# Later turns for the first key tiles, and four query products ahead of the later keys, in the projection stage of a two-layer encoder

## The chip, the cores and the metric

The kernel runs on one core of one Trainium2 chip. Its time is that of the whole program on the device, in microseconds; less is better. Five engines work side by side, each down its own queue in order: PE (matrix products and transposes), DVE, ACT and POOL (elementwise work and reductions), and SP, which issues the DMAs. They wait for each other on semaphores only.

## The reference

Two layers over 1024 tokens of 1024 channels, float32. Layer 0 mixes tokens by grouped-query attention, layer 1 by centred pooling; each layer then attends into a memory of 256 tokens and applies a gated MLP. The change lies in the first step of layer 0:

```python
h = rmsnorm(x, attn_norm)
qkv = h @ w_qkv                      # 16 query heads, 4 key heads, 4 value heads, 64 wide
q = apply_axial_rope(rmsnorm(q, q_gain), cos, sin) * HEAD_DIM ** -0.5
k = apply_axial_rope(rmsnorm(k, k_gain), cos, sin)
```

The scores, the softmax and all the rest follow from these q, k and v.

## The kernel before, in words

**Tiles.** Tokens come in eight tiles of 128. The projection makes, for each tile t, one product of 256 columns for the four key heads, ("K", t), one for the four value heads, ("V", t), and four for the query heads, (g, t), g being the group of four heads. `QKV` (line 41) is the list of these products in PE's order; the entries ("S", n) are score products that come later. Each product multiplies the tile's 1024 channels, eight blocks of 128, as float32 split into a high and a low part: three matmuls for each block (lines 761 to 763, `mm3`), 24 in all.

**Inputs.** The left side, `hT`, is x transposed, times the gain, split in two. It comes in four chunks of tokens, `CHUNKS`: tile 0, tile 1, tiles 2 and 3, tiles 4 to 7. `plan_columns(n)` loads chunk n from the transposed copy of x (DMA, L857) and splits it (L692 on ACT for the high part, L690 on DVE for the low). `plan_rows(t)` loads the rows of tile t (L929), squares and sums them on ACT (L933) and makes the row's normaliser `first[t]` on POOL (L935, L936); whatever follows a product of tile t multiplies by it. `plan_weights(piece, s)` loads 1 MB of weights in two DMAs (L948) and splits them (L674, L954). Raw tiles all go through six buffers, `scr`. `plan_tables` builds the tables of cosines and sines times the gains from one loaded table on POOL (L903, L910), for keys early on and for queries once key tile 0 is through its head.

**Head.** A key or query product goes through `plan_head`: square (ACT, L1011), sum (DVE, L1015), reciprocal root (POOL, L734 and L736), scale (DVE, L1023), two halves of the rotation (DVE, L1030 twice, L1034), and their sum (POOL, L1038). From tile 2 on a key tile also has a difference to the key two tiles back (POOL, L1056). Then comes its **turn**: PE transposes the result (L1062 for keys, two or four transposes; L1093 for queries, two), and ACT and DVE copy it out (L674, L677).

**Order.** `main` walks through `QKV` and hands each step to a planner (`Plan`). A turn is not placed right behind its product but `LAG` = 4 products later; `todo` holds the turns that are still to come. PE's order is exactly the order of these calls. For the other engines the planner works out when each operation is due so that PE is served in time, sorts by those times, and simulates the engines with costs of its own to fix the order in which instructions are written into each queue. So a step that moves on PE also changes the queues of ACT, DVE, POOL and SP; on the chip each engine then keeps to its written order.

Before the change, chunk 2 is planned once key tile 1 is, chunk 3 once key tile 3 is, and the rows of tile t + 1 behind key tile t:

```python
LAG = 4
...
if kind == "K" and t + 1 < NT:
    if t in (1, 3):
        plan_columns(t // 2 + 2)
    plan_rows(t + 1)
todo.append((count + LAG, after))
```

PE's order before therefore begins K0 K1 V0 V1 K2, turn of K0, V2, turn of K1, K3 V3 K4, turn of K2, the query products of tiles 0 and 1 of group 0, and so on, with turns between them. Some idle transposes (`IDLE`, L976) keep PE at work before the first products.

Of the kernel before, what the change touches and what calls it, by code (L numbers as in the profile page):

```python
# [37 lines left out]
LAST = S - (NPIECE - 1) * PIECE  # L38
MIXER = ("D0", "D1", "D2", "D3", "D4", "D5", "D6", "M0", "D7", "M1", "O0", "M2", "M3", "O2", "T0", "M4", "M5", "M6", "O4",
         "T2", "M7", "O1", "O6", "M8", "T4", "M9", "O3", "T6", "O5", "T1", "O7")  # L40
QKV = (("K", 0), ("K", 1), ("V", 0), ("V", 1), ("K", 2), ("V", 2), ("K", 3), ("V", 3),
       ("K", 4), (0, 0), (0, 1), ("K", 5), (0, 2), (0, 3), ("K", 6), (0, 4), (0, 5), ("K", 7), (0, 6), (0, 7),
       *(it for n in range(24) for it in ([(1 + n // 8, n % 8), ("S", n // 4)] if n % 4 == 1 else [(1 + n // 8, n % 8)])),
       ("S", 6), ("V", 4), ("S", 7), ("V", 5), ("V", 6), ("V", 7))
LAG = 4
QN = 4
POOLED = (2, 3)
GROUPS = [(half, m) for half in range(2) for m in range(NH // 2)]
# [587 lines left out]
class Kernel:  # L636
# [140 lines left out]
    def attention(self):  # L777
# [3 lines left out]
        K, dK = [R.get() for _ in range(2)], R.get()  # L781
        V = [R.get(), None]
# [44 lines left out]
        with tc.tile_pool(name="qk", bufs=1, reuse_waits="tile") as qk, self.psum("psq", 1, 6) as self.ps:  # L827
# [12 lines left out]
            def x_tile(n, j):  # L840
                at_ = (0, 1, 2, 4)[n] + j
                return a["xt"][at_].rearrange("p (k n) -> p k n", n=CHUNKS[n][1])

            def w_tile(piece, g):
                at_ = 2 * {"K": NKV, "V": NKV + 1, "late": NKV + 1}.get(piece, piece) + g
                return w[at_].rearrange("p (a b) -> p a b", a=4)

            def plan_columns(n):
                c0, w = CHUNKS[n]
                per = D // w  # L850
                for j in range(NK // per):
                    raw = ("xT", n, j)

                    def fetch(raw=raw, j=j):
                        at[raw] = self.scr().rearrange("p (k n) -> p k n", k=per)
                        if n:
                            nc.sync.dma_start(out=at[raw], in_=x_tile(n, j))  # L857

                    def part(lo, k, raw=raw, j=j):
                        hi, lo_ = (R.v(z, 4)[:, k % 4, c0 % 512:c0 % 512 + w] for z in hT[c0 // 512][2 * (k // 4):2 * (k // 4) + 2])  # L860
                        self.hi_lo_half(lo, hi, lo_, at[raw][:, k - per * j], gcol[:, k:k + 1])

                    def begin(g):
                        if not g:
                            nc.sync.dma_start(out=gcol, in_=a["gcol"])
                            fetch()
                        k4, r = slice(4 * g, 4 * g + 4), self.scr().rearrange("p (a b) -> p a b", a=4)
                        at["wraw", "K", g] = r
                        nc.sync.dma_start(out=at[raw][:, k4], in_=x_tile(0, 0)[:, k4])
                        for k in (slice(0, 2), slice(2, 4)):  # L870
                            nc.sync.dma_start(out=r[:, k], in_=w_tile("K", g)[:, k])
                    if n:
                        plan.add("load", 1, fetch, (), [raw], [("scr", raw)])
                    else:
                        for g in range(2):
                            k = ("wraw", "K", g)
                            plan.add("load", 1.3, partial(begin, g), (), [(raw, g), k] + ["gcol"] * (not g),
                                     [("scr", k)] + [("scr", raw)] * (not g), [raw], late=-21.0 + g)
                    for k in range(per * j, per * j + per):
                        key = ("hT", n, k)  # L880
                        src = raw if n else (raw, k // 4)
                        plan.add("copy", cost[w], partial(part, 0, k), [src, "gcol"], [key], uses=[raw])
                        plan.add("add", cost[w], partial(part, 1, k), [src, key, "gcol"], [key], uses=[raw])
                    if not n:
                        plan_weights("K", 0)
# [38 lines left out]
            def plan_rows(t):  # L924
                h, junk = ("h", t), ("hjunk", t)

                def fetch():
                    at[h] = self.scr()
                    nc.sync.dma_start(out=at[h], in_=xin[t * P:(t + 1) * P, :])  # L929

                def square():
                    ss = self.stat(1, "ss")
                    nc.scalar.activation(self.psA(), at[h], AF.Square, accum_out=ss)  # L933
                    ms = self.stat(1, "ms")
                    nc.gpsimd.tensor_scalar(ms, ss, 1.0 / D, EPS, op0=OP.mult, op1=OP.add)  # L935
                    nc.gpsimd.tensor_tensor(out=first[:, t:t + 1], in0=ms, in1=self.mh[:, :1], op=OP.pow)  # L936
                plan.add("load", 1, fetch, (), [h], [("scr", h)], late={0: -1.0, 1: 5.0, 2: 3.0}.get(t, -4.0))
                plan.add("square", 1024, square, [h], [("first", t)], [("A", junk)], [h])
# [52 lines left out]
            def plan_v(t, b):  # L991
                src = lambda: at[b].rearrange("p (h c) -> p h c", h=4)

                def part(j):
                    if V[t // 4] is None:
                        V[t // 4] = R.get()
                    v = R.tiles[V[t // 4]].rearrange("p (k h c) -> p k h c", k=4, h=4)[:, t % 4]
                    self.hi_lo_half(j, v[:, :, :HD], v[:, :, HD:], src(), first[:, t:t + 1])
                own = [("first", t)]
                plan.add("copy", 360, partial(part, 0), [b] + own, [("V", t)], uses=[b], room=None if t < 4 else ("V1", 2))  # L1000
                plan.add("add", 340, partial(part, 1), [b, ("V", t)] + own, [("V", t)], uses=[b])
# [129 lines left out]
            def main():  # L1131
                todo, count = [], 0
                plan_columns(0)
                plan_columns(1)
                plan_rows(0)
                plan_tables("K")
                for it in QKV:
                    kind, t = it[0], it[-1]
                    if kind == "S":
                        plan_peaks(t)  # L1140
                        continue
                    if kind == "V":
                        if t == 0:
                            plan_weights("V", 1)
                        elif t == 4:
                            plan_weights("late", 0)
                        done = t == NT - 1
                        b = plan_gemm(it, "V" if t < 4 else "late", t, (lambda: R.put(*hT[1])) if done else (lambda: None),
                                      ("half", 8) if done else None)
                        plan_v(t, b)  # L1150
                        after = None
                    elif kind == "K":
                        after = plan_k(t, plan_gemm(it, "K", t))
                        if t == 0:
                            plan_tables("Q")
                    else:
                        g, half = it[0], t // 4
                        if not t:
                            plan_weights(g, (2, 1, 0, 1)[g])
                        ended, gives = [], 0  # L1160
                        if it == (0, NT - 1):
                            ended, gives = sets[2], 4
                        elif it == (NKV - 1, 3):
                            ended, gives = hT[0], 8
                        it = half, *it
                        after = plan_q(it, plan_gemm(it, g, t, lambda ended=ended: R.put(*ended), ("half", gives) if gives else None))
                    count += 1
                    if kind == "K" and t + 1 < NT:
                        if t in (1, 3):
                            plan_columns(t // 2 + 2)  # L1170
                        plan_rows(t + 1)
                    todo.append((count + LAG, after))
                    while todo and todo[0][0] <= count:
                        f = todo.pop(0)[1]
                        if f:
                            f()
                for _, f in todo:
                    if f:
                        f()
                plan.run()  # L1180

            with tc.manual_schedule():
                idle = self.psB()
                for _ in range(WARM):
                    nc.tensor.transpose(idle[:, :P], self.ident, self.ident)
                main()
# [1219 lines left out]
```

## Time and profile before

| | |
|---|---|
| median of three runs | 2414.16 us (2412.76 to 2416.49) |
| the profiled execution | 2419.23 us, span 2417.4 us |
| granted PE clock, mean | 0.997 |
| PE busy | 2392.6 us, 99% of the span |
| the projections | to about 160 us |

Rows of a timeline begin with the start in us from the span's start and the duration in us; then come engine, line and operation, the tile written and those read, and in brackets the time that the engine sat idle before, with what ended it. A table of stretches gives for each the busy us of each engine with the number of instructions, then the granted PE clock, the DMA engines' busy share and GB/s. A row of a group gives the count, the busy time in us, the mean of one in ns, and the idle time before them.

### The profile page before, as it was taken

The numbers are of one execution on the slowest core, as the hardware profiler recorded it, in microseconds if no ns is written. First come the engines' busy times: TensorE is split into PE (matmuls) and PEld (weight loads), VectorE is DVE, ScalarE is ACT, GpSimd is POOL, SyncE is SP. The second block draws the span as 40 slices with busy tenths as digits, with TensorE's granted clock in tenths as the row PEclk, the third lists the DMA queues.
The fourth block names the chain that finished last, engine by engine and source line by source line (L and its number), as shares of the span: only waits on it lengthen the run. The fifth ranks groups of instructions, "written<-read, shape, count | busy, mean of one in ns | idle before, by whom it ended". The sixth has DMA issues, their size and how long they took to land.

```text
span 2417.4 us, 33999 instructions
## 1 busy us (share of the span) xinstructions
PE 2392.6 (99%) x12484; PEld 1939.3 (80%) x12484; DVE 1887.3 (78%) x2689; ACT 1182.0 (49%) x1894; POOL 426.1 (18%) x465
## 2 busy tenths in 40 slices
PE   8999999999999999999999999999999999999998
PEld 8984544688998888888888888798888888887887
DVE  6789999549873798888887767987389888888875
ACT  6335556425562555455454427555255554545442
POOL 6757777410010000000000003011000000000001
PEclk9999999999999999999999999999999999999999
DMA  7000001425951234333387533696123332338852
GB/s 254 19 2 10 19 15 45 139 89 191 322 199 44 88 98 129 109 88 109 103 288 243 190 100 124 205 324 216 51 86 113 105 109 87 114 119 272 261 187 101
DMA packets 323004, 324.41 MB, mean 134 GB/s; under 512 B 32533, under 2 KB 253053, under 8 KB 322837
## 3 DMA queue, kind: packets, MB, share of 16 engines
q1 hardware_dynamic: 322837, 322.23, 41.5%
q8 instruction: 99, 1.62, 0.3%
q14 instruction: 68, 0.56, 0.1%
HBM read 234.58 MB, written 82.64 MB: 131 GB/s over the span
## 4 chain that ended last, share of the span: by engine, by line
PE 90%; DVE 3%; issue 3%; DMA 2%; POOL 1%; ACT 1%; SPq 0%; POOLq 0%; DVEq 0%; ACTq 0%
PE pB L761 23%; PE pB L763 23%; PE pB L762 22%; PE pO L1267 4%; PE pT L1225 3%; PE pA L763 3%; PE pA L761 3%; PE pA L762 3%; PE pS L799 2%; DVE R L677 1%; PE pB L330 1%; PE pS L1303 1%; PE pA L2282 0%; DMA scr<-X 0%; DMA scr<-in_ffn_w_down 0%
## 5 line engine op out<-in xcount | busy, mean ns | idle before, releaser
L761 PE MATMUL pB<-R,R 128*128 128x512 f32 (+1 forms) x2764 | 1026.0, 371 | 3.7 <-DVE scr L446 1.2
L763 PE MATMUL pB<-R,R 128*128 128x512 f32 (+1 forms) x2760 | 1018.3, 369 | 1.4 <-DVE R L677 1.2
L762 PE MATMUL pB<-R,R 128*128 128x512 f32 (+1 forms) x2764 | 1019.3, 369 | 0.2 <-DVE R L677 0.2
L761 PEld LDWEIGHTS pB<-R,R 128*128 128x128 f32 x2764 | 522.6, 189 | 95.4 <-DVE scr L446 2.5
L763 PEld LDWEIGHTS pB<-R,R 128*128 128x128 f32 x2760 | 521.8, 189 | 89.5 <-DVE R L677 3.2
L762 PEld LDWEIGHTS pB<-R,R 128*128 128x128 f32 x2764 | 522.8, 189 | 86.3 <-DVE R L677 1.2
L674 ACT ACTIVATE R<-scr 128x512 fp32r<-128x512 f32 (+3 forms) x372 | 268.7, 750 | 230.6 <-DMA scr<-Gs 59.3
L734 POOL TENSOR_SCALAR ms<-ss 128x1 f32<-128x1 f32 (+2 forms) x93 | 26.0, 280 | 1655.6 <-ACT R L742 1284.1
L677 DVE TENSOR_TENSOR R<-X,R 128x512 fp32r<-128x512 f32 x374 | 253.1, 689 | 67.8 <-ACT R L674 67.2
L677 DVE TENSOR_TENSOR R<-scr,R 128x512 fp32r<-128x512 f32 (+2 forms) x332 | 283.8, 884 | 25.7 <-ACT R L674 25.1
L674 ACT ACTIVATE R<-X 128x512 fp32r<-128x512 f32 x374 | 231.9, 630 | 133.4 <-PE pB L762 64.0
L444 ACT COPY scr<-pB 128x512 f32<-128x512 f32 x156 | 91.1, 584 | 180.1 <-PE pB L763 172.9
L805 DVE TENSOR_REDUCE nm<-pS 128x1 f32<-128x512 f32 x240 | 152.9, 684 | 18.2 <-PE pS L799 16.4
L1970 DVE TENSOR_TENSOR X<-pB,X 128x512 f32<-128x512 f32 (+1 forms) x145 | 99.4, 687 | 82.3 <-PE pB L763 81.2
L1232 ACT ACTIVATE X<-pT 128x1024 f32<-128x1024 f32 x128 | 125.2, 1023 | 76.6 <-PE pT L1225 73.0
L761 PE MATMUL pA<-R,R 128*128 128x512 f32 (+1 forms) x420 | 150.6, 358 | 0.0
L763 PE MATMUL pA<-R,R 128*128 128x512 f32 (+1 forms) x420 | 150.2, 358 | 0.0
L762 PE MATMUL pA<-R,R 128*128 128x512 f32 (+1 forms) x420 | 150.0, 357 | 0.0
L1267 PE MATMUL pO<-X,X 128*64 128x512 f32 x512 | 123.8, 605 | 0.0
L446 DVE TENSOR_TENSOR scr<-pB,scr 128x512 f32<-128x512 f32 x156 | 107.2, 687 | 11.5 <-PE pB L763 11.4
L1225 PE MATMUL pT<-R,R 64*128 64x512 f32 x768 | 104.7, 393 | 1.3 <-ACT X L1232 1.3
L1815 DVE SCALAR_TENSOR_TENSOR scr<-scr,conv 128x1023 f32<-128x1023 f32 x66 | 84.7, 1284 | 20.9 <-ACT scr L1810 18.9
(179 smaller groups left out, 2882.3 us busy)
## 6 DMA issues: line engine op xcount, KB each, us to landing
X<-in_ffn_w_up SPq DMA_DIRECT2D x82, 512.0 KB
Gs<-X SPq DMA_DIRECT2D x105, 256.0 KB
scr<-in_ffn_w_down SPq DMA_DIRECT2D x45, 512.0 KB
scr<-Gs SPq DMA_DIRECT2D x35, 512.0 KB
scr<-in_xattn_w_kv SPq DMA_DIRECT2D x32, 512.0 KB
scr<-Gs SPq DMA_DIRECT2D x42, 384.0 KB
Wt<-scr SPq DMA_DIRECT2D x44, 256.0 KB
Gs<-scr SPq DMA_DIRECT2D x42, 256.0 KB
```

What stands on the lines that cost most here:

```text
L444: self.nc.scalar.copy(out, p)
L446: self.nc.vector.tensor_tensor(out=out, in0=p, in1=out, op=OP.add)
L674: self.nc.scalar.activation(hi, src, AF.Copy)
L677: self.nc.vector.tensor_tensor(out=lo, in0=src, in1=hi.bitcast(F32), op=OP.subtract)
L761: mm(out, ah, bh, start=start, stop=False)
L762: mm(out, ah, bl, start=False, stop=False)
L763: mm(out, al, bh, start=False, stop=stop)
L805: nc.vector.tensor_reduce(NM[G][:, 2 * n + x.start:2 * n + x.stop], S, axis=AX.X, op=OP.max, negate=True)
L1225: nc.tensor.matmul(T[G, kt % 2][:, x * 512:(x + 1) * 512], left, right, start=first and (i, j) == (0, 0), stop=shifted or (not first and i ...
L1232: nc.scalar.activation(E[G, kt], T[G, kt % 2], AF.Exp)
L1267: nc.tensor.matmul(O[G][x * HD:(x + 1) * HD], V32[kt // 4][:, kt % 4, m // 4 * 2 + x], E[G, kt][:, x * 512:(x + 1) * 512], start=kt == 0, ...
L1970: nc.vector.tensor_tensor(out=x, in0=banks[b][:, c], in1=x, op=OP.add)
```

## The change

In `QKV` key tile 3 moves ahead of value tile 2, and the query products of group 0 for tiles 0 to 3 move ahead of key tiles 4 to 7, which then alternate with the query products of tiles 4 to 7. The turns of key tiles 0 to 3 come six products after their own (`EARLY`), those of all others four as before. Chunk 3 of the columns, and the rows of tile 4, are planned behind the second query product instead of behind key tile 3; the loads of the query weights thus come ahead of them in the plan. PE's order becomes K0 K1 V0 V1 K2 K3 V2, turn of K0, V3, turn of K1, three query products, turn of K2, the fourth, turn of K3, K4, the first query's turn, and so on. The set of instructions is the same. Lines of the new file behind line 1166 stand five lower.

```diff
-QKV = (("K", 0), ("K", 1), ("V", 0), ("V", 1), ("K", 2), ("V", 2), ("K", 3), ("V", 3),
-       ("K", 4), (0, 0), (0, 1), ("K", 5), (0, 2), (0, 3), ("K", 6), (0, 4), (0, 5), ("K", 7), (0, 6), (0, 7),
+QKV = (("K", 0), ("K", 1), ("V", 0), ("V", 1), ("K", 2), ("K", 3), ("V", 2), ("V", 3),
+       (0, 0), (0, 1), (0, 2), (0, 3), ("K", 4), (0, 4), ("K", 5), (0, 5), ("K", 6), (0, 6), ("K", 7), (0, 7),
...
-LAG = 4
+LAG, EARLY = 4, 6
...
                     if kind == "K" and t + 1 < NT:
-                        if t in (1, 3):
-                            plan_columns(t // 2 + 2)
-                        plan_rows(t + 1)
-                    todo.append((count + LAG, after))
+                        if t == 1:
+                            plan_columns(2)
+                        if t != 3:
+                            plan_rows(t + 1)
+                    if it == (0, 0, 1):
+                        plan_columns(3)
+                        plan_rows(4)
+                    todo.append((count + (EARLY if kind == "K" and t < 4 else LAG), after))
+                    todo.sort(key=lambda x: x[0])
```

## The prediction

> **What bounds the kernel now.** I read first the page's busy times, then the table of stretches over the projection stage, then PE's timeline where that table shows a hole.
>
> ```profile
> PE 2392.6 (99%) x12484; PEld 1939.3 (80%) x12484; DVE 1887.3 (78%) x2689; ACT 1182.0 (49%) x1894; POOL 426.1 (18%) x465
> ```
> ```profile
> core 0: us, PE busy (x) PEld busy (x) DVE busy (x) ACT busy (x) POOL busy (x), PEclk, DMA share, GB/s
> 10.00:20.00 10.00, 9.05 (x75) 8.85 (x76) 6.93 (x15) 8.20 (x19) 4.16 (x7) 1.00 0.94 346
> ...
> 60.00:160.00 100.00, 100.00 (x827) 97.14 (x826) 77.19 (x199) 29.91 (x71) 71.85 (x99) 1.00 0.04 12
> ...
> 25.53:28.94 3.41, 0.59 (x6) 0.39 (x4) 2.34 (x8) 2.54 (x6) 2.20 (x5) 1.00 0.90 300
> 28.94:32.35 3.41, 2.64 (x13) 2.64 (x14) 3.28 (x7) 2.57 (x5) 2.56 (x6) 0.50 0.34 132
> 32.35:35.77 3.42, 3.42 (x18) 3.42 (x18) 3.13 (x7) 1.93 (x5) 3.25 (x4) 0.50 0.50 161
> 35.77:39.18 3.41, 3.41 (x31) 3.41 (x31) 3.41 (x5) 1.85 (x4) 3.41 (x6) 1.00 0.70 223
> ...
> 438.50:441.95 3.45, 2.12 (x14) 0.86 (x12) 2.78 (x3) 2.11 (x5) 2.92 (x3) 1.00 0.85 298
> ```
> ```profile
> 25.84 0.28 PE L763 MATMUL pB<-T,R 128*128 128x256 f32 x1
> 29.71 0.69 PE L1062 MATMUL pB<-ident,kr 128*128 128x128 f32 x2 [3.59 <-POOL kr L1038]
> ...
> 35.32 0.60 PE L1062 MATMUL pB<-ident,kr 128*128 128x128 f32 x2
> ...
> 56.59 0.38 PE L1062 MATMUL pB<-ident,kr 128*128 128x128 f32 x2
> 56.80 0.38 PE L1062 MATMUL pB<-ident,dk 128*128 128x128 f32 x2
> 59.90 0.38 PE L1093 MATMUL pB<-ident,qn 128*128 128x128 f32 x2
> ```
>
> PE is busy 99% of the span, so only its holes can be won. In the projections there is one: after K2's product (last matmul 25.84, done about 25.96) PE waits 3.59 us for POOL's last add on key tile 0 (L1038), because K0's turn (L1062) stands next in its queue. Then the granted clock is 0.50 from 28.94 to 35.77: from K0's turn to K1's (29.71 to 35.32) one product and two transposes take 5.61. At full speed key tile 4's turn and a product take 59.90 - 56.59 = 3.31, of which two transposes are 56.80 - 56.59 = 0.21: a product is 3.31 - 0.42 = 2.89, and that stretch would take 3.10. The half clock costs 2.5. So the hole is worth 6.1 us at most, 0.25% of the run. From 36 to 160 PE is full: the next thing to be late was nothing.
>
> POOL and DVE are next, with 71.85 and 77.19 of the 100 us from 60 to 160.
>
> **The change, part by part.** PE's matmuls are the same, reordered; the built programs' later stages have the same order on every engine, so whatever is won or lost is settled by about 60 us and carried to the end.
>
> (a) K0's turn moves behind K3's and V2's products: PE reaches it at 25.96 + 2 x 2.89 = 31.7. At its old ready time (add at 28.93 + 0.72) the wait would be gone.
>
> (b) But the planner, given later due times, sets the other queues anew, and K0's chain is late too. On SP the two tiles of the third chunk of columns now stand ahead of row tile 1, the rotary table and the gains; on ACT their eight splits stand ahead of the square of row tile 0 (L933), on which K0's scale waits.
>
> ```profile
> 14.73 1.06 ACT L674 ACTIVATE R<-scr 128x1024 fp32r<-128x1024 f32 x1 [0.25 <-DMA scr<-in_attn_w_qkv]
> 15.70 1.01 ACT L933 ACTIVATE pA<-scr 128x1024 f32<-128x1024 f32 x1
> 16.65 0.19 ACT L933 ACTIVATION_READ_ACCUMULATOR pA<-scr 128x1 f32 x1
> 17.79 0.47 ACT L1011 ACTIVATE sq<-pB,first 128x256 f32<-128x256 f32 x1 [0.95 <-POOL first L936]
> ...
> 21.33 3.31 ACT L692 ACTIVATE R<-scr,gcol 128x256 fp32r<-128x256 f32 x8 [1.61 <-DMA scr<-in_xt]
> ```
> ```profile
> 17.72 1.31 POOL L903 TENSOR_TENSOR scr<-tab,gk 128x512 f32<-128x512 f32 x1
> 18.99 0.88 POOL L910 TENSOR_TENSOR scr<-tab,gk 128x128 f32<-128x128 f32 x2
> ...
> 20.86 0.19 POOL L734 TENSOR_SCALAR ms<-ss 128x4 f32<-128x4 f32 x1
> 21.13 1.02 POOL L736 TENSOR_TENSOR rs<-ms,mh 128x4 f32<-128x4 f32 x1
> 22.11 1.16 POOL L910 TENSOR_TENSOR scr<-tab,gk 128x128 f32<-128x128 f32 x2
> ```
>
> V's weights land at 14.7; at 346 GB/s a 512 KB tile takes 1.5, so the two tiles land at 16.2 and 17.7 (estimates), not before 21.33, and the splits (8 in 3.31) end at 19.5. Square of row 0, 1.15 (15.70 to 16.84, with its read-out): 20.7; POOL's two steps for it, 0.9 (they lie between 16.84 and the cosines at 17.72): 21.6; K0's square 0.5, then row 1's 1.15: 23.2; POOL 0.9: 24.1. From there POOL has all its inputs and works down its queue: K's cosines 1.31, K0's rstd 1.3, row 2's 0.8, K's four sines 2.04, K1's rstd 1.3, row 3's 0.8, K0's add 0.74: 32.4. **K0's wait** is 32.4 - 31.7 = 0.7 instead of 3.59; K1's rstd and add then make K1's turn wait about 1.2 (K2's rstd 1.3 and K1's add 0.74 stand behind K0's, with DVE's weight splits beside them).
>
> (c) The four query products follow, needing no keys. Their weights' loads go ahead of the last chunk on SP; that chunk's eight 512-column splits on DVE, needed by K4's product, now stand right ahead of the first query's scale (L1023). The place that decides is the first query's turn (L1093). In PE's queue 13 products and four key turns stand ahead of it, not 14 and five: PE saves 3.31 up to there and owes it after. So with T the end of POOL's add for that query, and 0.1 from there to PE:
>
> change = T + 0.1 + 3.31 - 59.90 + (half clock, if any).
>
> ```profile
> L736 POOL TENSOR_TENSOR rs<-ms,mh 128x4 f32<-128x4 f32 x6 | 6.6, 1099 | 0.5
> L1038 POOL TENSOR_TENSOR kr<-kr,rb 128x256 f32<-128x256 f32 x5 | 4.1, 824 | 0.8 <-DVE kr L1034 0.7
> L936 POOL TENSOR_TENSOR first<-ms,mh 128x1 f32<-128x1 f32 x6 | 4.1, 684 | 0.5
> L734 POOL TENSOR_SCALAR ms<-ss 128x4 f32<-128x4 f32 x6 | 3.2, 535 | 0.5
> L910 POOL TENSOR_TENSOR tab<-tab,gq 128x128 f32<-128x128 f32 x4 | 2.9, 764 | 0.0
> L935 POOL TENSOR_SCALAR ms<-ss 128x1 f32<-128x1 f32 x6 | 2.3, 384 | 4.8 <-ACT pA L933 4.6
> L1056 POOL TENSOR_TENSOR dk<-kr 128x256 f32<-128x256 f32 x3 | 2.2, 739 | 0.1
> ```
> ```profile
> 30.60 0.74 POOL L1038 TENSOR_TENSOR kr<-kr,rb 128x256 f32<-128x256 f32 x1 [0.68 <-DVE kr L1034]
> ...
> 41.08 1.06 POOL L734 TENSOR_SCALAR ms<-ss 128x4 f32<-128x4 f32 x1
> ...
> 43.84 1.10 POOL L935 TENSOR_SCALAR ms<-ss 128x1 f32<-128x1 f32 x1 [0.59 <-ACT pA L933]
> ...
> 47.34 0.19 POOL L935 TENSOR_SCALAR ms<-ss 128x1 f32<-128x1 f32 x1 [0.77 <-ACT pA L933]
> 47.62 0.55 POOL L936 TENSOR_TENSOR first<-ms,mh 128x1 f32<-128x1 f32 x1
> ...
> 57.26 0.74 POOL L1038 TENSOR_TENSOR qn<-qn,rb 128x256 f32<-128x256 f32 x1
> ```
>
> Before, POOL went from 26.45 to 58.0 (57.26 + 0.74) through that list: 31.55 us, with three idle gaps of 0.68 + 0.59 + 0.77 = 2.04. Worked without gaps it is 29.5. After, K4's add and difference (1.5, with spacing 1.65) drop out of it, and K's cosines, sines and K0's rstd, done before 26.45 in the old order, come in: 1.31 + 2.04 + 1.3, with spacing 4.9. So T = 24.1 + 29.5 - 1.65 + 4.9 = **56.9**.
>
> PE meanwhile: K0's turn at 32.4 takes 0.2, V3 2.9, the wait 1.2, K1's turn 0.2, three queries 8.7, K2's turn 0.4, the fourth query 2.9: 48.9. K3's turn needs POOL's second difference, in the same queue: none to 1.6 of wait; I take 1 (it only comes off the wait that follows). With that turn, 0.4, and K4's product PE stands at the query's turn at 53.2 and waits 56.9 - 53.2 = 3.7, as long as the old wait. Without half clock: 56.9 + 0.1 + 3.31 - 59.90 = +0.4.
>
> Bounds of T: the means of the group stand above the short rows by 6 x (0.535 - 0.19) for L734, 6 x (1.10 - 1.02) for L736, 5 x (0.82 - 0.74) for L1038, 6 x (0.68 - 0.55) for L936, 6 x (0.38 - 0.19) for L935 and 4 x (0.76 - 0.44) for L910: 6.3 in all. With all steps at their shortest T is 50.6; if the old gaps of 2.0 come again, 58.9. I take 56.9 because the same DVE splits stand beside the same POOL steps.
>
> (d) **The half clock comes back.** Before, a wait of 3.59 brought it on, with PE busy 0.59 in the 3.41 us ahead of the drop; at 438.50 a stretch with 2.12 busy kept the full clock. The bound lies between 1.3 and 2.8 idle in 3.41, and a wait of 3.7 is over it wherever it falls. The price: one such stretch at half rate, 3.41 x 0.45 = 1.5, to two, 3.0; the old one was 2.5. I take 2.4.
>
> The Trainium skill, TensorE: Matmul & The Clock Gate, Part 1, says half rate comes after at least one idle window of about 3.4 us, in windows that run free. The row at 25.53 does not fully agree: the clock fell after a stretch with 0.59 busy. Read strictly, a wait of 3.7 would seldom fill a window, and the sum would stay at +0.4.
>
> (e) Covers. SP: the last chunk lands later; its splits end on DVE a little ahead of K4's product, and should they be late, each us is taken from the wait at the query's turn, 3.7 deep. PSUM: V2's product needs K0's bank, free once K0 is scaled, about 27, two us ahead.
>
> **Sum**: +0.4 + 2.4 = +2.8 us. The profiled execution took 2419.23 (span 2417.4), the median of the runs is 2414.16; both move by 2.8: 2422.0 and **2417.0**. A measurement of this kernel can tell some 0.2% from no change, 4.8 us; the three runs spread over 3.7.
>
> **The rivals.**
> Faster: POOL keeps up. The old hole goes and none opens. PE without the waits in (b) and (c), 0.7 + 1.2 + 1, reaches the query's turn at 50.3: 50.3 + 3.31 - 59.90 = -6.3, 2407.9. For it: POOL's shortest rows give T = 50.6. Against: POOL was never that fast beside DVE's splits. To win over 4.8 T must stay under 51.7: 0.08.
>
> The clock holds: as forecast, but the wait at the query's turn stays short of the bound, or the page's strict rule is true: +0.4, 2414.6. Within the same class; 0.15.
>
> Slower: DVE holds POOL. The eight splits stand right ahead of the query's scale, and beside such splits POOL's steps grew (41.08: 1.06 for 0.19, DVE running a weight split). If POOL finds the old gaps again and some more, T = 59.2, and the half clock lasts two stretches, 3.0: 59.2 + 0.1 + 3.31 - 59.90 + 3.0 = +5.7, 2419.9. It decides from T + half clock = 61.3. For it: POOL's queue is in order, and any late input holds all behind it. 0.30.
>
> That the change does not move the turn can be left out: the built order has K0's turn behind V2.
>
> **How the numbers follow.** My forecast of +2.8 has 0.47, the clock that holds 0.15, slower 0.30, faster 0.08. Same is 0.47 + 0.15 = 0.62. The range: low end, T = 54 without half clock, -2.5, with a little of the faster rival and the runs' spread, 2410.5; high end, the slower rival with 1.6 of the spread, 2421.5.
>
> **What would show it.** K0's turn waits under 1.5 us at 31.7, not 3.59; no half clock around 30; a wait of 3 to 4 us for POOL's L1038 at about 53 ahead of the first L1093 (five lines lower in the new file), the clock at 0.50 behind it until about 60; from there to 160 PE full. I am wrong if that turn starts before 54 (then faster), or after 59 (then slower), or if PE has a hole after 65.

## The result, and the profile after

| | before | after |
|---|---|---|
| median of 17 runs each | 2414.12 us (2411.61 to 2418.83) | 2420.45 us (2417.84 to 2423.63) |
| ratio after / before | | 1.0023 (1.0016 to 1.0030) |
| profiled execution, span | 2419.23, 2417.4 us | 2418.70, 2416.9 us |

By the ratio the change costs 0.23%, some 5.6 us; the two medians lie 6.3 apart. The forecast was +2.8, on the right side, at half the size. The two profiled executions say the opposite: after is 0.5 us shorter. So the first thing to read is how far each trace has come at the end of the projections. The view by source line gives it for their score products (L799): durations, then the first and last start. The first row is before, the second after.

```profile
L799 PE MATMUL pA<-R,R x16: 492/498/501, 85.5 to 160.3; 64*128 64x512 f32 x16
L799 PE MATMUL pA<-R,R x16: 492/498/501, 87.3 to 162.4; 64*128 64x512 f32 x16
```

At 162.4 against 160.3 after is 2.1 us late, and 1.8 of them are there at the first of these products. So most of the loss lies ahead of 85 us. This is PE's timeline of after, cut to the four places where it waited and the matmuls ahead of the first and the last, and the stretches around the last:

```profile
31.66 0.28 PE L763 MATMUL pB<-R,R 128*128 128x256 f32 x1
33.31 0.44 PE L1062 MATMUL pB<-ident,kr 128*128 128x128 f32 x2 [1.36 <-POOL kr L1038]
...
37.47 0.44 PE L1062 MATMUL pB<-ident,kr 128*128 128x128 f32 x2 [0.84 <-POOL kr L1038]
...
50.82 0.44 PE L1062 MATMUL pB<-ident,dk 128*128 128x128 f32 x2 [0.75 <-POOL dk L1056]
...
53.67 0.28 PE L762 MATMUL pB<-T,R 128*128 128x256 f32 x1
57.23 0.69 PE L1093 MATMUL pB<-ident,qn 128*128 128x128 f32 x2 [3.17 <-POOL qn L1038]
```
```profile
53.59:57.00 3.41, 0.48 (x5) 0.27 (x3) 2.45 (x7) 0.47 (x1) 3.08 (x6) 1.00 1.00 407
57.00:60.41 3.41, 3.17 (x15) 3.18 (x16) 2.21 (x8) 2.27 (x3) 2.93 (x6) 0.50 0.07 29
60.00:160.00 100.00, 100.00 (x825) 97.14 (x824) 75.43 (x195) 30.44 (x73) 70.38 (x99) 1.00 0.05 17
```

The old hole at 26 us is gone. In its place stand short waits at the turns of key tiles 0, 1 and 3, and one of 3.17 us at the first query's turn, with one stretch at half clock behind it. From 60 to 160 PE is full, as before.

Why the keys are late shows on ACT and POOL, timelines of after:

```profile
16.55 3.31 ACT L692 ACTIVATE R<-scr,gcol 128x256 fp32r<-128x256 f32 x8 [1.26 <-DMA scr<-in_xt]
19.77 1.01 ACT L933 ACTIVATE pA<-scr 128x1024 f32<-128x1024 f32 x1
```
```profile
23.46 0.19 POOL L935 TENSOR_SCALAR ms<-ss 128x1 f32<-128x1 f32 x1 [1.63 <-ACT pA L933]
23.73 0.56 POOL L936 TENSOR_TENSOR first<-ms,mh 128x1 f32<-128x1 f32 x1
24.67 1.29 POOL L903 TENSOR_TENSOR scr<-tab,gk 128x512 f32<-128x512 f32 x1 [0.38 <-DMA gk<-in_attn_k_gain]
...
32.49 0.76 POOL L1038 TENSOR_TENSOR kr<-kr,rb 128x256 f32<-128x256 f32 x1
```

The third chunk's splits stand ahead of the square of row tile 0, and the cosines (L903) start at 24.67 instead of 17.72. Two things hold them there, almost to the same moment. POOL comes to them at 24.29, since row tile 1's normaliser, which waits for ACT, now stands ahead of them; then the gains land 0.38 later.

What remained open was 3.5 of the 5.6 us (5.6 less the 2.1 that the two traces show), and which part of the change is to blame.

### The profile page after: what moved, and what is told of

Same layout as the page of the kernel before. It is cut to its first block, busy times and chain, and to the rows that moved or that the text cites. A ratio compares the mean times of both kernels' runs of the same rounds, so it can differ in the third digit from the quotient of the medians.

```text
span 2416.9 us, 33997 instructions
## 1 busy us (share of the span) xinstructions
PE 2390.8 (99%) x12484; PEld 1937.1 (80%) x12484; DVE 1886.9 (78%) x2689; ACT 1182.0 (49%) x1894; POOL 425.2 (18%) x465
## 4 chain that ended last, share of the span: by engine, by line
PE 90%; DVE 3%; issue 3%; POOL 2%; DMA 2%; ACT 1%; SPq 0%; POOLq 0%; DVEq 0%; ACTq 0%
PE pB L761 23%; PE pB L763 22%; PE pB L762 22%; PE pO L1272 4%; PE pT L1230 3%; PE pA L763 3%; PE pA L761 3%; PE pA L762 3%; PE pS L799 2%; PE pB L330 1%; DVE R L677 1%; PE pS L1308 1%; POOL rs L736 0%; DMA scr<-in_ffn_w_down 0%; DMA scr<-X 0%
## 5 line engine op out<-in xcount | busy, mean ns | idle before, releaser
L677 DVE TENSOR_TENSOR R<-X,R 128x512 fp32r<-128x512 f32 x374 | 252.5, 687 | 67.6 <-ACT R L674 66.9
L677 DVE TENSOR_TENSOR R<-scr,R 128x512 fp32r<-128x512 f32 (+2 forms) x332 | 284.3, 885 | 23.7 <-ACT R L674 23.1
L1230 PE MATMUL pT<-R,R 64*128 64x512 f32 x768 | 105.2, 393 | 1.4 <-ACT X L1237 1.4
```

Of the source, the lines that this page charges most:

```text
L677: self.nc.vector.tensor_tensor(out=lo, in0=src, in1=hi.bitcast(F32), op=OP.subtract)
L1230: nc.tensor.matmul(T[G, kt % 2][:, x * 512:(x + 1) * 512], left, right, start=first and (i, j) == (0, 0), stop=shifted or (not first and i ...
```

## The experiments

**Before and after once more.** Both kernels unchanged, for other profiles of them.

> The kernel before, unchanged, against itself. Both theories ask how much of the gap of the medians (+6.3 us: 2420.45 against 2414.12) the two traces can show: they show +2.1 us on the tensor engine by 65 us, which stays to 490 us. Theory W (an unlucky profile): the profiled execution of before (2419.23, above all its other runs) lost more than its usual share: two half-clock stretches behind the hole at 26 us (2.5 us by the prediction), one more at 1489.8 (1.5 us) and two chance waits at 490 and 1236 us (0.66 and 0.77). Then another profile of the same kernel has its last score product of the projections (L799) 1 to 3 us earlier than 160.3 us, and fewer half-clock stretches. Rival S (it is always so): the hole at 26 us is again 3.5 to 3.7 us with two stretches behind it and the last L799 stands at 160.2 to 160.4; then the missing 3.5 us lie in later stages. Median near 2414 under both.

The ratio of before to itself is 1.0000 (0.9991 to 1.0009), the new profile's span 2409.9. Its timelines, PE and ACT:

```profile
27.36 0.44 PE L1062 MATMUL pB<-ident,kr 128*128 128x128 f32 x2 [1.65 <-POOL kr L1038]
```
```profile
19.26 3.31 ACT L692 ACTIVATE R<-scr,gcol 128x256 fp32r<-128x256 f32 x8 [0.69 <-DMA scr<-in_xt]
```

The hole is 1.65 us, not 3.59: the third chunk landed about 2 us earlier, its splits began at 19.26, not 21.33. No half clock follows, and the last score product starts at 156.8. Theory W holds: the profile that I predicted from was the odd one.

> One more profile of the kernel before, for the size of its hole at the first key's turn. Theory W (the hole follows the landing of the third chunk of columns, on which ACT's splits wait: landed and begun at 21.33, hole 3.59; at 19.26, hole 1.65): the two move together again, hole = 1.65 + 0.94 x (start of those splits - 19.26) within 0.4 us. Rival V (the hole's size has another source on POOL or DVE): it does not fit that line.

```profile
27.68 0.69 PE L1062 MATMUL pB<-ident,kr 128*128 128x128 f32 x2 [2.02 <-POOL kr L1038]
```
```profile
19.29 3.31 ACT L692 ACTIVATE R<-scr,gcol 128x256 fp32r<-128x256 f32 x8
```

The line asks for 1.68, measured 2.02: within the 0.4, but two of the three points lie together, so this is weak support. Nor did ACT wait for the chunk this time. Most of the 0.34 above the line is one POOL step ahead of the add: a normaliser (L936) took 0.85 us, 0.55 in the second profile. A stretch of half clock followed. Last score product: 157.5.

> The changed kernel, unchanged, once more. Theory W (the profiled execution of before was the odd one: its third chunk of columns landed 2 us late, and the second profile of before has a hole of 1.65 instead of 3.59 us and its tensor engine 3.6 us further at the end of the projections, 156.3 against 159.9): the changed kernel's wait at the first query's turn stands in every execution, 3 to 4 us at 53 to 58, the matmuls of the last score product of the projections (L799) again at 161 to 163, and the time 2419 to 2421.5, 5 to 7 us above before. Rival C (chance): its waits scatter as much as those of before, and a second profile has the wait at the first query's turn under 2 us and no half clock behind it; the time then reaches down to 2415.

Ratio 1.0024 (1.0015 to 1.0033), median 2419.33. The wait is there again:

```profile
56.73 0.44 PE L1093 MATMUL pB<-ident,qn 128*128 128x128 f32 x2 [3.15 <-POOL qn L1038]
```

But no half clock follows it, and the last score product starts at 160.5. So after is at 162.4 and 160.5, before at 160.3, 156.8 and 157.5. Against the two other profiles of before, mean 157.15, after is 3.4 to 5.3 us late, which is most of the gap of 5.6 to 6.3. The rest of the span, from there to the end, is 2254.5 and 2256.0 in after, 2257.1, 2253.1 and 2254.8 in before: the means differ by 0.3, but with a scatter of 4 a share of the later stages of 1 or 2 us could not be seen.

**Which part of the change.** Each part alone.

```diff
-LAG, EARLY = 4, 6
+LAG, EARLY = 4, 4        # queries_only: new order of products and new places of the loads, old turns
```

> The new order of the products, but all turns four products later, as before: EARLY = 4. Theory T (the later key turns cost the time: with later due times the planner puts the third chunk of columns ahead of the rows and the rotary table, and the keys' chain on POOL starts 5 us later): the chain starts as in before, the hole at the first key's turn is there again, 3.4 us, but no wait at the first query's turn; the time is that of before within 1 us (2413 to 2415), some 6 us below the changed kernel. Rival Q (the four query products ahead of the later keys cost it: more steps for POOL before the first query's turn, and the splits of the last chunk ahead of its scale): a wait of about 3 us at the first query's turn stays, on top of the hole at 26 us: 2419 to 2422.

2412.61, ratio 0.9995 (0.9986 to 1.0004); last score product at 158.0. There was a hole of 1.33 at the first key's turn and none at the first query's. The four query products ahead of the keys cost nothing.

```diff
 # late_turns: on the kernel before, QKV and the loads' places untouched
-LAG = 4
+LAG, EARLY = 4, 6
...
-                    todo.append((count + LAG, after))
+                    todo.append((count + (EARLY if kind == "K" and t < 4 else LAG), after))
+                    todo.sort(key=lambda x: x[0])
```

> The old order of the products and the old places of the loads, but the first four key tiles are turned six products later: EARLY = 6. Theory T: the planner puts the third chunk of columns ahead of the rows and the table here too; the keys' chain is late as in the changed kernel, the last chunk's loads stand behind it, and key tile 4's product, now right behind the turns, waits for its columns, 3 to 6 us in all: 2416 to 2420. Rival Q: with the hole at 26 us gone and nothing in its place this part alone gains: 2409 to 2412.

2420.09, ratio 1.0029 (1.0018 to 1.0039). The size is Theory T's upper end, the place isn't. PE's timeline, its two longest waits:

```profile
40.23 0.55 PE L761 MATMUL pB<-T,R 128*128 128x256 f32 x1 [1.93 <-DVE kr L1023]
...
47.40 0.58 PE L762 MATMUL pB<-R,R 128*128 128x256 f32 x1 [2.52 <-DVE R L954]
```

A product waits until DVE's late scale frees its bank, another for the query weights' splits; not for the columns. Each wait has a stretch of half clock behind it. The chain begins as in the change: POOL's cosines started at 26.55, after 2.87 us of waiting for the gains. Later turns of the four keys alone cost the whole 0.2 to 0.3%.

**Which queue.** First the planner is told of the old due times; PE keeps the order of the change.

```diff
-plan.add("scale", 2.4, both, [qn, rb], [qn] + [("kr", t)] * (kind == "K"), uses=[qn, rb])
+plan.add("scale", 2.4, both, [qn, rb], [qn] + [("kr", t)] * (kind == "K"), uses=[qn, rb], late=10.0 if kind == "K" and t < 4 else None)
```

> The changed kernel with one hint to the planner: the adds (L1038) of key tiles 0 to 3 are due 10 us after their products' place, as with turns four products later, though the turns stand six later, as in the change. The tensor engine's order is that of the changed kernel, instruction for instruction; only the other queues go back (the loads to rows, table and gains ahead of the third chunk). Theory P (the planner's later due times cost the time, not the order of the products): the first key's turn waits under 0.5 us, the first query's turn under 3, and the time is that of before or below it: 2411 to 2414.5. Rival O (the order itself costs it, since the first query's turn comes too early for POOL's sum of work): the wait at the first query's turn stays above 3 us with half clock behind it: 2417 to 2420.

2411.86, ratio 0.9991 (0.9982 to 1.0000), 7.5 us below the changed kernel run beside it (2419.33), with the same order on PE. All key turns were met without a wait, and the first query's waited 0.61:

```profile
50.53 0.44 PE L1093 MATMUL pB<-ident,qn 128*128 128x128 f32 x2 [0.61 <-POOL qn L1038]
```

So not the order of the products, but what the planner made of the later due times.

```diff
-plan.add("load", 1.1, load, (), ["tab", "gQ", "gK"])
+plan.add("load", 1.1, load, (), ["tab", "gQ", "gK"], late=2.0)
```

> The changed kernel with one other hint: the load of the rotary table and the gains is due 2 us after the plan's start. On SP it then stands ahead of the third chunk of columns again, as in before; nothing is said to the planner of the keys' adds, which stay due as late as in the change. Theory L (what costs the time is that the keys' tables load behind the third chunk of columns, so that POOL starts the cosines at 24.7 instead of 17 us and all of its queue is late): the cosines start at 17 to 18.5, the first key's turn waits under 0.5 us, the first query's turn under 2.5, and the time falls by 4 to 7 us against the changed kernel, to 2412.5 to 2416. Rival R (the order of POOL's and ACT's own queues under the later due times): the cosines start early, but the add of the first query still ends at 56 to 58; 2418 to 2421.

2414.41, ratio 1.0004 (0.9995 to 1.0012). Here the due times of the keys are as late as in the change, and only the tables' load is told to come early. ACT, POOL and PE:

```profile
15.21 1.01 ACT L933 ACTIVATE pA<-scr 128x1024 f32<-128x1024 f32 x1
```
```profile
17.66 1.30 POOL L903 TENSOR_TENSOR scr<-tab,gk 128x512 f32<-128x512 f32 x1 [0.19 <-DMA gk<-in_attn_k_gain]
```
```profile
53.14 0.44 PE L1093 MATMUL pB<-ident,qn 128*128 128x128 f32 x2 [1.73 <-POOL qn L1038]
```

Theory L's numbers came: the cosines start 7 us earlier, the first query's turn 4.1 us earlier than in the first profile of after, and the loss is gone. But the hint moved other queues too. ACT's square of row tile 0 is back ahead of the third chunk's splits, at 15.21 instead of 19.77, and POOL's cosines ahead of row tile 1's normaliser. In the trace of after the load alone held the cosines for 0.38 us only; in that order of ACT and POOL they could not have started before 24.29, and with that landing of the gains not before 24.67. By these rows it took both, the load's place and the order of ACT and POOL, and the planner moves them together. How the loss splits between them is not shown.

**What held the first query's turn.** POOL and DVE in the timeline of after, ahead of it:

```profile
52.74 0.20 POOL L734 TENSOR_SCALAR ms<-ss 128x4 f32<-128x4 f32 x1
53.02 1.02 POOL L736 TENSOR_TENSOR rs<-ms,mh 128x4 f32<-128x4 f32 x1
54.13 0.20 POOL L734 TENSOR_SCALAR ms<-ss 128x4 f32<-128x4 f32 x1
54.41 1.01 POOL L736 TENSOR_TENSOR rs<-ms,mh 128x4 f32<-128x4 f32 x1
55.50 0.19 POOL L935 TENSOR_SCALAR ms<-ss 128x1 f32<-128x1 f32 x1
55.78 0.56 POOL L936 TENSOR_TENSOR first<-ms,mh 128x1 f32<-128x1 f32 x1
56.30 0.88 POOL L1038 TENSOR_TENSOR qn<-qn,rb 128x256 f32<-128x256 f32 x1
```
```profile
52.22 0.41 DVE L1034 TENSOR_TENSOR qn<-qn,tab 128x256 f32<-128x256 f32 x1
```

The add's last operand is there at 52.63; two other queries' roots and a row's normaliser stand ahead of it, and it ends at 57.18.

```diff
-plan.add("scale", 2.9, rstd, [ss], [ss])
+plan.add("scale", 2.9, rstd, [ss] + ([f"qn{(0, 0, 0)}"] if it in ((0, 0, 1), (0, 0, 2)) else []), [ss])
```

> The changed kernel, where the planner is told that the reciprocal roots (L734, L736) of the second and third query wait for the first query's add (L1038). In POOL's queue the add then stands ahead of them, and key tile 3's add behind the first query's root. Theory O (POOL's written order holds the first query's turn: in the trace of the changed kernel the add's operands are there at 52.6 us, but two roots of other queries and a row's normaliser stand ahead of it until 56.3): the add ends at 51 to 53.5 us, the wait of 3.2 us at the first query's turn shrinks to under 1.6, no half clock behind it, and the time falls by 1.5 to 4 us against the changed kernel: 2416.5 to 2419. Rival D (DVE's eight splits of the last chunk, or POOL's sum of work, set the end of the add): the add ends at 56 to 58 as before and the time stays at 2420 to 2421.

2417.68, ratio 1.0012 (1.0003 to 1.0021): about half the loss is gone, though this interval and those of after (1.0016 to 1.0030, 1.0015 to 1.0033) overlap. The add moved even further than expected, and PE got less of it:

```profile
48.75 1.18 POOL L1038 TENSOR_TENSOR qn<-qn,rb 128x256 f32<-128x256 f32 x1 [0.69 <-DVE qn L1034]
```
```profile
54.24 0.66 PE L1093 MATMUL pB<-ident,qn 128*128 128x128 f32 x2 [1.33 <-DVE R L677]
55.34 0.58 PE L761 MATMUL pB<-R,R 128*128 128x256 f32 x1 [0.44 <-DVE qn L1023]
```

With POOL out of the way, DVE is next late, with the copy out of an earlier turn (L677), queued behind the last chunk's splits. And the half clock, which should have stayed away, came for two stretches, the second from 57.57 to 60.99:

```profile
50.75:54.16 3.41, 2.06 (x12) 1.38 (x11) 3.12 (x7) 2.75 (x6) 1.36 (x4) 1.00 0.83 281
54.16:57.57 3.41, 2.89 (x12) 2.53 (x13) 1.47 (x5) 3.05 (x6) 2.91 (x7) 0.50 0.89 278
```

So in this profile the turn starts 2.5 to 3.0 us earlier than in the two profiles of after, but the last score product, at 161.4, lies between theirs. That POOL's order held the turn is shown; the gain of an earlier add is not, beyond the median.

**The half clock.**

```diff
-                        at[b] = self.psB()[:, :256]
+                        at[b], spare = (lambda z: (z[:, :256], z[:, 256:256 + P]))(self.psB())
...
+                    for _ in range(24 if it == ("K", 4) else 0):
+                        nc.tensor.transpose(spare, self.ident, self.ident)
```

> The changed kernel with 24 idle transposes (0.107 us each, 2.6 us in all) behind key tile 4's product, in the unused half of its bank, so that the tensor engine works during its wait for the first query's add. They add no wait: the add ends about 3.3 us behind that product. Theory H (the half clock behind the wait is a cost of its own, 1.5 us in the trace of the changed kernel): no half clock at 57, and the time falls by 1 to 3 us against the changed kernel. Rival N (POOL sets the pace behind it anyway, so that the slower products only fill later waits): the clock stays up, but the time stays within 0.7 us of the changed kernel.

The transposes filled the wait (0.54 was left of it) and the clock stayed up at 57, but the median is 2419.96, ratio 1.0022 (1.0013 to 1.0030), beside 2419.33 for the changed kernel on the same chip. Rival N's number, but not by its mechanism: in the second profile of after the clock held as well. What is not paid in every execution can't show much in a median, so this run does not settle the half clock's price. The traces do better: from the start of the first query's turn to the last score product it is 105.2 us in the first profile of after, with the half clock, and 103.8 in the second and here, without it. One stretch costs 1.4 us, and POOL does not swallow it.

**A better version?**

```diff
-LAG, EARLY = 4, 6
+LAG, EARLY = 4, 5        # with late=10.0 on the keys' adds
```

> As the run before this one, with the same hint, but the first four key tiles are turned five products later instead of six. Theory P: both holes close, the first key's turn by one product of cover (2.9 us against a hole of 1.3 to 3.6) and the first query's turn because one more product stands behind it than ahead; the projections end 1 to 2 us earlier than in before: 2410.5 to 2413. Rival O: a wait of 2 us or more stays at the first query's turn or the next one: 2414 to 2418.

2413.40, ratio 0.9994 (0.9985 to 1.0003). No wait at either turn, but 0.96 at a later product for its bank.

> The changed kernel with the adds of key tiles 0 to 3 due as before, once more, to see whether it beats before as well: its ratio was 0.9991 (0.9982 to 1.0). Theory G (a real gain: the hole of 1.65 to 3.6 us at the first key's turn and the wait of 1.1 for the query weights' splits are gone, and the projections ended at 154.0 against 156.3 us): 1.5 to 3 us below before, ratio 0.9988 to 0.9994. Rival Z (chance of the first round): within 1 us of before, ratio 0.9996 to 1.0004.

2414.04, ratio 0.9999 (0.9990 to 1.0008): Rival Z. The third chunk's splits began at 20.17 in this profile, and the first query's turn waited 2.04, with a stretch of half clock behind it. The due times put back undo the loss; a gain over before is not shown.

## Why the prediction was right, and where it was off

**(a) right.** PE is through with V2 at 31.95 (31.7 forecast), where K0's turn waits.

**(b) right, with one term left out, and the heart of the matter.** The splits end at 19.86 (19.5 forecast), POOL starts the cosines at 24.67 (24.1), K0's add ends at 33.25 (32.4). The waits: K0 1.36 (0.7), K1 0.84 (1.2), K3 0.75 (1). The step came to the cosines by ACT's queue alone, which brings POOL there at 24.29. That the gains land later still, which the step had on SP's list but put at nothing, cost 0.38. The hint on the tables' load, with what it moved on ACT and POOL, brings the time to that of before.

**(c) right.** T = 57.18 (56.9 forecast); PE is there at 54.05 (53.2) and waits 3.17 (3.7). The formula gives 57.18 + 0.1 + 3.31 - 59.90 = +0.7. I summed POOL's work and overlooked that two steps of other queries need not stand ahead of the add; the sum fitted because they do.

**(d) mis-sized, and not always there.** One stretch at half rate, not 2.4 us: 2.1 at the last score product less 0.7 is 1.4. In the second profile of after there was none, with the same wait. There the clock held, as in the rival of that name. That a wait of 3.7 is over the bound "wherever it falls" did not follow from the step's own numbers: split evenly over two windows it leaves 1.85 us idle in each, within the 1.3 to 2.8 in which the step had left the bound open.

**The base was wrong**, and this is the step that failed in size: "both move by 2.8". The formula subtracts 59.90, the start of the first query's turn in the profiled execution of before. I had 2419.23 against 2414.16 on the table and took the 5 us as lying evenly on both sides. Some 3.4 of them sat ahead of that turn, in the hole and the half clock behind it. In the other two profiles of before that turn starts at 56.3 and 56.7; these are the view by source line of L1093:

```profile
L1093 PE MATMUL pB<-ident,qn x64: 270/272/273, 56.3 to 166.3; 128*128 128x128 f32 x64
```
```profile
L1093 PE MATMUL pB<-ident,qn x64: 270/272/329, 56.7 to 167.0; 128*128 128x128 f32 x64
```

With their mean the formula gives 57.18 + 0.1 + 3.31 - 56.5 = +4.1 without half clock, and 1.4 more with it: 5.5 for the first profile of after. For the second, whose turn starts at 56.73, it gives 56.73 + 3.31 - 56.5 = +3.5. The ratio shows 5.6: the right base covers most of it, and 1 to 2 us in an average execution stay open. The changed kernel's wait did not move like this between its two profiles: 3.17 and 3.15.

**The rivals.** DVE holding POOL gave nearly the measured time, 2419.9, by a mechanism that wasn't there: T was 57.2, not 59.2. POOL keeping up did not come. The measured time lies near the top of the range, which had been drawn that wide for the rival of DVE: that it fell inside is in part luck. Of the two statements at the end, the turn's start between 54 and 59 and no hole after 65 hold. (Two slips that move nothing: L1093 keeps its number in the new file, and the excess of the means over the short rows adds up to 6.2, not 6.3.)

**The page of the Trainium skill.** By its strict rule, TensorE: Matmul & The Clock Gate, Part 1, a wait of 3.7 would seldom bring half rate. That windows run free fits: the same wait brought it in one profile of after and not in the other. That a window must be idle does not: the third profile of before fell to half rate behind one with 1.41 of 3.41 busy (last section).

## What to carry to other kernels

Where a planner orders several queues from due times, a step moved on one engine moves loads on another: look at what each queue puts ahead of the step's earliest input, and give the planner the old due time if only the one engine's order is to change. Before pricing a hole, set the profiled execution beside the median: a run that stands 5 us above it carries its excess somewhere, here two thirds of it in the very wait that was being priced. Then ask which load sets that wait, and whether the change still depends on it. And when a hint puts one load back, compare all queues before the load is called the cause.

## What the runs showed of the hardware

The granted clock changes at the ends of windows of 3.41 us, and whether a wait of 2 to 3.5 us halves it depended on how the wait fell across them. In the second profile of after, the wait of 3.15 lay across two windows, half in each, and the clock held:

```profile
51.80:55.21 3.41, 1.78 (x16) 1.57 (x14) 1.57 (x6) 1.62 (x3) 2.98 (x6) 1.00 1.03 414
55.21:58.62 3.41, 1.89 (x16) 1.89 (x17) 2.15 (x8) 1.41 (x3) 3.17 (x5) 1.00 0.50 203
58.62:62.03 3.41, 3.41 (x31) 3.41 (x31) 2.96 (x12) 1.61 (x3) 2.80 (x6) 1.00 0.00 0
```

In the third profile of before a wait of only 2.02 lay within one, and it fell:

```profile
24.26:27.67 3.41, 1.41 (x13) 1.20 (x11) 2.35 (x8) 2.34 (x6) 2.97 (x6) 1.00 0.92 336
27.67:31.08 3.41, 3.40 (x16) 3.40 (x17) 3.38 (x7) 3.41 (x7) 2.56 (x4) 0.50 0.05 17
```

Busy time alone does not sort the windows: the one of add_first with 2.06 us busy, but only 12 matmuls, fell too, while those with 1.78 and 1.89 busy and 16 matmuls each held.

And the landing of one chunk moved by some 2 us between executions of the same kernel (its splits, waiting for it, began at 19.26 in one and at 21.33 in the other; its first issue on SP came only 0.4 us later, 12.25 against 11.88), and the hole behind it went from 1.65 to 3.59 us.
